# Moving every transfer of a log-softmax backward kernel from the sync engine's queue to GpSimd's software queue

## The chip, the cores and the metric

The kernel runs on one core of one Trainium2 chip. The metric is device time in microseconds (us), lower is better. Most executions of one kernel agree within 0.3%. All runs quoted here were at full granted clock. A transfer (DMA) is spread over 16 transfer engines of the core; the trace does not name them, so "the first" and "the last" engine below are meant in order of arrival. "SP" is the sync engine (SyncE), "DVE" VectorE, "ACT" ScalarE, "POOL" GpSimd.

## The reference

```python
batch, seq_len, vocab = 8, 1024, 8192            # float32
softmax_x = np.exp(y)
sum_dy = np.sum(dy, axis=-1, keepdims=True)
return (dy - softmax_x * sum_dy).astype(np.float32)
```

It reads two tensors of 268 MB and writes one of the same size.

## The kernel before

The 8192 rows are handled in 32 groups of 256: each of the 128 partitions holds two neighbouring rows (R = 2) of D = 8192 columns. `dy` of a group is one 8 MB transfer, `y` is two of 4 MB, and the result is written over `dy` in SBUF and stored as one 8 MB transfer. There are two `dy` buffers and two `y` buffers, together 192 KB of each partition. So a `dy` load must wait until the store from the same buffer, two groups back, has landed.

```python
    dyp = ctx.enter_context(tc.tile_pool(name="dyp", bufs=2))
    yp = ctx.enter_context(tc.tile_pool(name="yp", bufs=R))

    def load_dy(g):
        dy_t = dyp.tile([P, R * D], fp32, name="dy_t")
        nc.sync.dma_start(out=dy_t[:], in_=dy_v[g])
        s_t = stats.tile([P, R], fp32, name="s_t")
        nc.vector.tensor_reduce(...)              # s_t = -sum of each row of dy, L47

    def load_y(g):
        for r in range(R):
            y_t = yp.tile([P, D], fp32, name="y_t")
            nc.sync.dma_start(out=y_t[:], in_=y_v[g][:, r * D : (r + 1) * D])

    def compute(dy_t, s_t, y_ts):                 # per row: two halves of 4096 columns
        ...
                nc.scalar.activation(e, e, EXP)   # L69
                nc.vector.scalar_tensor_tensor(   # dy += exp(y) * s_t, L70, "the product"
                    out=d, in0=e, scalar=s_t[:, r : r + 1], in1=d, op0=ALU.mult, op1=ALU.add
                )

    # ... loop: load_y(g); compute(g); load_dy(g + 1); store(g).
    # The last groups are handled a little differently.
```

All transfers go through one queue, in the order y, y, dy of the next group, store, and every engine works through its share of each transfer in that order (the packets of the trace come in it).

## Time and profile before

| | before |
|---|---|
| time, median of the first 4 runs | 1867.24 us |
| moved, rate over the span | 805.36 MB, 432 GB/s |
| one group's packets on one engine | 16 of 64 KB at 2.418 us and 16 of 32 KB at 1.213 us: 58.1 us |
| loop period | 58.08 us |

The page of the kernel before. The second line is the busy time of each compute engine, with its share of the span; the row of digits is the busy share of the transfer engines in 40 slices, in tenths (9 is 90% or more); the line that begins with q1 is the hardware queue, with its share of the 16 engines' time; the last three lines are groups of instructions, with busy time and mean ns of one, then idle time before them and what ended it.

```profile
span 1865.4 us, 712 instructions
DVE 1119.2 (60%) x160; ACT 457.1 (25%) x129; POOL 0.2 (0%) x4
...
DMA  9999999999999999999999999999999999999999
...
q1 hardware_dynamic: 18576, 805.31, 99.9%
...
L70 DVE SCALAR_TENSOR_TENSOR dy_t<-y_t,s_t,dy_t 128x4096 f32<-128x4096 f32 x128 | 568.1, 4481 | 490.3 <-ACT y_t L69 490.1
L69 ACT ACTIVATE y_t<-y_t 128x4096 f32<-128x4096 f32 x128 | 455.9, 3608 | 1375.6 <-DMA y_t<-in_y_dram 1375.6
L47 DVE TENSOR_REDUCE s_t<-dy_t 128x2 f32<-128x16384 f32 x32 | 551.0, 17220 | 232.1 <-DMA dy_t<-in_dy_dram 232.1
```

The transfer engines are busy from beginning to end and the compute engines are not. The idle times of the last three lines are waits for loads, directly or through ACT. The kernel is bound by the transfers.

The timeline of the kernel before in the middle of the run (start, length, engine, line, operation; in brackets how long the engine stood idle and for what):

```profile
977.93 8.88 DVE L70 SCALAR_TENSOR_TENSOR dy_t<-y_t,s_t,dy_t 128x4096 f32<-128x4096 f32 x2 [0.83 <-ACT y_t L69]
986.84 0.34 SPq L77 DMA_DIRECT2D out_dram<-dy_t  x1
987.28 0.86 SPq L60 DMA_DIRECT2D y_t<-in_y_dram  x2
993.56 17.22 DVE L47 TENSOR_REDUCE s_t<-dy_t 128x2 f32<-128x16384 f32 x1 [6.75 <-DMA dy_t<-in_dy_dram]
1012.91 0.33 SPq L45 DMA_DIRECT2D dy_t<-in_dy_dram  x1
...
1044.92 0.34 SPq L77 DMA_DIRECT2D out_dram<-dy_t  x1
```

The last products end at 986.81, the store is issued at once, the y loads of the next group behind it. The `dy` load ahead of them in the queue has landed in full only at 993.56, 6.75 us later, when the reduction starts. So the queue still holds work when the store joins it. The chain of waits of the same stretch repeats every 58.08 us; its largest pieces are these (start, length, what):

```profile
929.66 44.53 DMA y_t<-in_y_dram
...
987.75 44.52 DMA y_t<-in_y_dram
...
1045.83 44.52 DMA y_t<-in_y_dram
```

They are waits for y, but of a y load that stands in the queue behind the store: a wait for bandwidth and not for latency.

### The profile page before, as it was taken

The numbers are of one execution on the slowest core, as the hardware profiler recorded it, in microseconds if no ns is written. First come the engines' busy times: TensorE is split into PE (matmuls) and PEld (weight loads), VectorE is DVE, ScalarE is ACT, GpSimd is POOL, SyncE is SP. The second block draws the span as 40 slices with busy tenths as digits, with TensorE's granted clock in tenths as the row PEclk, the third lists the DMA queues.
The fourth block names the chain that finished last, engine by engine and source line by source line (L and its number), as shares of the span: only waits on it lengthen the run. The fifth ranks groups of instructions, "written<-read, shape, count | busy, mean of one in ns | idle before, by whom it ended". The sixth has DMA issues, their size and how long they took to land.

```text
span 1865.4 us, 712 instructions
## 1 busy us (share of the span) xinstructions
DVE 1119.2 (60%) x160; ACT 457.1 (25%) x129; POOL 0.2 (0%) x4
## 2 busy tenths in 40 slices
DVE  5675555755557555575555755657656576565664
ACT  2123321233212332123321233212332113331132
POOL 0000000000000000000000000000000000000000
DMA  9999999999999999999999999999999999999999
GB/s 427 416 434 431 443 433 422 435 437 436 427 433 431 440 430 434 431 429 441 433 437 425 433 442 431 434 425 436 438 434 433 428 434 437 437 431 430 429 435 396
DMA packets 18582, 805.36 MB, mean 432 GB/s; under 512 B 2064, under 2 KB 2064, under 8 KB 2064
## 3 DMA queue, kind: packets, MB, share of 16 engines
q1 hardware_dynamic: 18576, 805.31, 99.9%
q14 instruction: 6, 0.05, 0.0%
HBM read 536.87 MB, written 268.44 MB: 432 GB/s over the span
## 4 chain that ended last, share of the span: by engine, by line
DMA 74%; DVE 17%; ACT 6%; SPq 1%; issue 1%; DVEq 0%; ACTq 0%
DMA y_t<-in_y_dram 69%; DVE dy_t L70 15%; ACT y_t L69 6%; DMA dy_t<-in_dy_dram 3%; DVE s_t L47 2%; DMA out_dram<-dy_t 1%; SPq L60 1%; SPq L77 1%; DVEq L122 0%; ACTq L69 0%; DVEq L70 0%
## 5 line engine op out<-in xcount | busy, mean ns | idle before, releaser
L70 DVE SCALAR_TENSOR_TENSOR dy_t<-y_t,s_t,dy_t 128x4096 f32<-128x4096 f32 x128 | 568.1, 4481 | 490.3 <-ACT y_t L69 490.1
L69 ACT ACTIVATE y_t<-y_t 128x4096 f32<-128x4096 f32 x128 | 455.9, 3608 | 1375.6 <-DMA y_t<-in_y_dram 1375.6
L47 DVE TENSOR_REDUCE s_t<-dy_t 128x2 f32<-128x16384 f32 x32 | 551.0, 17220 | 232.1 <-DMA dy_t<-in_dy_dram 232.1
L69 ACT ACT_TABLE_LOAD x1 | 1.3, 1283 | 0.7 <-PEq L111 0.7
L111 POOL MEMSET const-bfloat16-1.0<- 128x1 bf16 x1 | 0.1, 102 | 0.0
L111 POOL MEMSET const-uint8-127<- 128x1 uint8 x1 | 0.1, 102 | 0.0
L111 POOL MEMSET const-float32-1.0<- 128x1 f32 x1 | 0.1, 99 | 0.0
L111 POOL MEMSET const-float32-0.0<- 128x1 f32 x1 | 0.1, 98 | 0.2 <-issue 0.2
## 6 DMA issues: line engine op xcount, KB each, us to landing
y_t<-in_y_dram SPq DMA_DIRECT2D x64, 4096.0 KB, 35.9
out_dram<-dy_t SPq DMA_DIRECT2D x2, 4096.0 KB, 22.6
dy_t<-in_dy_dram SPq DMA_DIRECT2D x32, 38.7
out_dram<-dy_t SPq DMA_DIRECT2D x31, 26.1
```

The lines of the kernel that those rows point to most:

```text
L47: nc.vector.tensor_reduce(out=s_t[:], in_=dy_t[:].rearrange("p (r d) -> p r d", r=R), axis=mybir.AxisListType.X, op=ALU.add, negate=True,)
L60: nc.sync.dma_start(out=y_t[:], in_=y_v[g][:, r * D : (r + 1) * D])
L69: nc.scalar.activation(e, e, EXP)
L70: nc.vector.scalar_tensor_tensor(out=d, in0=e, scalar=s_t[:, r : r + 1], in1=d, op0=ALU.mult, op1=ALU.add)
L77: nc.sync.dma_start(out=out_v[g][:, k * w : (k + 1) * w], in_=dy_t[:, k * w : (k + 1) * w])
L111: nc = _bacc.Bacc("TRN2", target_bir_lowering=False, num_devices=1)
```

## The change

All three kinds of transfer are issued from GpSimd. Their descriptors (what tells an engine what to copy) are then written by software on GpSimd and not by hardware. Bytes, order, sizes and buffers stay.

```diff
-        nc.sync.dma_start(out=dy_t[:], in_=dy_v[g])
+        nc.gpsimd.dma_start(out=dy_t[:], in_=dy_v[g])
...
-            nc.sync.dma_start(out=y_t[:], in_=y_v[g][:, r * D : (r + 1) * D])
+            nc.gpsimd.dma_start(out=y_t[:], in_=y_v[g][:, r * D : (r + 1) * D])
...
-            nc.sync.dma_start(
+            nc.gpsimd.dma_start(
                 out=out_v[g][:, k * w : (k + 1) * w], in_=dy_t[:, k * w : (k + 1) * w]
             )
```

## The prediction

> **What bounds the kernel now.** The transfers. The page of the kernel before shows 805.36 MB in a span of 1865.4 us (432 GB/s), the hardware queue at 99.9% of the 16 engines' span, and a 9 in every slice of the DMA row, against 60% for VectorE and 25% for ScalarE. The trace's packets: 8064 of 65,536 bytes at a median of 2.418 us and 8448 of 32,768 bytes at 1.213 us. One group of 256 rows costs each engine 16 of the former and 16 of the latter, 58.1 us; the chain of waits repeats every 58.08 us. The engines have almost no gap.
>
> **How the loop keeps the queue full (timeline, 930 to 1050 us).** A group's store is issued at 986.84, after VectorE's last product; the dy load ahead of it in the queue lands only at 993.56. So the store has 6.7 us of backlog in front of it. The y loads follow within 1.2 us and have the store's 19.4 us in front. The next dy load waits for that store to land (1012.91) and has two y loads, 19.4 us, in front. The chain of waits names y loads for 69% of the span, but this is queueing, not latency.
>
> **What the change does.** It removes 129 issues from SyncE, 0.33 to 0.4 us each in the timeline, and adds 129 on GpSimd, which otherwise does 0.2 us of work. Bytes, row lengths, order and buffers stay. I expect the same packets at the same 2.42 and 1.21 us, under a software queue. The Trainium skill, "DMA: Bandwidth & Descriptors", section "Latency and other measured facts", gives about 1 us to the first byte on the software path and 0.6 us on the hardware path; this trace has no software transfer to check it. Estimated from this page, the extra 0.4 us per issue, and even 2 us, is under the 6.7 us of the tightest place, so the steady loop hides it. It shows only at the first load (0.5 to 3 us, with any first-use cost on GpSimd) and at the end.
>
> "SBUF — State Buffer" in the skill describes descriptor writing locked out while VectorE runs a two-port fast mode. I take no instruction here to be in one (the product takes 4.44 us for 4096 columns, the reduction 1.05 ns per column). And the issues fall where VectorE is idle: the store and y loads in the 6.75 us between last product and reduction, the dy load after the reduction ended (1010.8).
>
> **Sum.** 1866.9 + about 2 at start and end + 0 to 0.1 us per group for fetching descriptors from memory (0 to 3) = about 1870 us; 8 times in 10 within 1863 to 1892. Faster by over 2%: 0.01; within 2%: 0.85; slower by over 2%: 0.14.
>
> **What would show it right.** A software queue with near 18,576 packets of the same sizes, 9 in all DMA slices, about 431 GB/s; a loop period of 58.1 to 58.3 us; the reduction's wait for dy still near 6.75 us; store issue to landing still near 26 us.
>
> **What would make it wrong.** Packets cut smaller, so that a fixed cost per packet appears; some of the 16 engines slower than others, because they also serve the descriptor rings; a stall at each transfer's end before the next begins (four transfers per group: 0.3 us each would be 2%); descriptor writing over 6 us per transfer, so that the store reaches a dry queue; or a long first use of GpSimd's software. Each would show as gaps or longer packets in the DMA row, and each makes it slower, not faster.

## The result, and the profile after

The kernel after takes 1878.38 us in the median (1877.34 to 1879.35, 4 runs) against 1867.24 us (1866.81 to 1868.3, 4 runs): 11.1 us more. The ratio is 1.0059 with a 95% interval of 1.0041 to 1.0076, so it is the same within 2%, but the small loss is real. Ratios here are the mean time of one kernel's fast runs over that of the other's of the same rounds, so not quite the ratio of the medians.

The page of the kernel after, the same lines and the one of the store's issue:

```profile
span 1877.6 us, 712 instructions
DVE 1119.2 (60%) x160; ACT 457.1 (24%) x129; POOL 68.4 (4%) x133
...
DMA  9999999999999999999999999999999999999998
...
q0 software_dynamic: 18576, 805.31, 99.7%
...
L70 DVE SCALAR_TENSOR_TENSOR dy_t<-y_t,s_t,dy_t 128x4096 f32<-128x4096 f32 x128 | 568.2, 4481 | 491.2 <-ACT y_t L69 491.0
L69 ACT ACTIVATE y_t<-y_t 128x4096 f32<-128x4096 f32 x128 | 455.9, 3608 | 1386.8 <-DMA y_t<-in_y_dram 1386.8
L47 DVE TENSOR_REDUCE s_t<-dy_t 128x2 f32<-128x16384 f32 x32 | 551.0, 17220 | 242.0 <-DMA dy_t<-in_dy_dram 242.0
L77 POOL DMA_DIRECT2D out_dram<-dy_t x33 | 17.7, 538 | 1009.3 <-DVE dy_t L70 1009.3
```

The queue is now the software queue q0. It holds the same bytes in the same 18,576 packets, at 99.7%. Compute is unchanged. The digits of the transfer row still read 9: the loss is too small for this view. The waits moved a little: ACT's for y by 11.2 us (1375.6 to 1386.8), the reduction's for dy by 9.9 us (232.1 to 242.0).

The chain of waits is of little use here. Its summary by engine in the kernel after begins:

```profile
issue 85%; DMA 9%; POOL 3%; DVE 2%; ACT 0%; POOLq 0%; DVEq 0%; PEldq 0%; ACTq 0%
```

"Issue" means time for which the view found nothing to wait for. GpSimd's issues now stand in the chain as instructions, and the view does not follow the waits of GpSimd's own queue further. It is not a new cost.

The timeline after, at about the same place:

```profile
932.33 0.54 POOL L77 DMA_DIRECT2D out_dram<-dy_t  x1 [31.49 <-DVE dy_t L70]
...
939.88 17.22 DVE L47 TENSOR_REDUCE s_t<-dy_t 128x2 f32<-128x16384 f32 x1 [7.85 <-DMA dy_t<-in_dy_dram]
...
982.32 8.88 DVE L70 SCALAR_TENSOR_TENSOR dy_t<-y_t,s_t,dy_t 128x4096 f32<-128x4096 f32 x2 [0.84 <-ACT y_t L69]
991.50 0.54 POOL L77 DMA_DIRECT2D out_dram<-dy_t  x1 [31.50 <-DVE dy_t L70]
992.02 1.05 POOL L60 DMA_DIRECT2D y_t<-in_y_dram  x2
998.13 17.22 DVE L47 TENSOR_REDUCE s_t<-dy_t 128x2 f32<-128x16384 f32 x1 [6.92 <-DMA dy_t<-in_dy_dram]
1017.68 0.53 POOL L45 DMA_DIRECT2D dy_t<-in_dy_dram  x1 [24.61 <-DMA out_dram<-dy_t]
...
1049.72 0.54 POOL L77 DMA_DIRECT2D out_dram<-dy_t  x1 [31.51 <-DVE dy_t L70]
...
1056.86 17.22 DVE L47 TENSOR_REDUCE s_t<-dy_t 128x2 f32<-128x16384 f32 x1 [7.44 <-DMA dy_t<-in_dy_dram]
```

Two things are to be seen. The last products end at 991.20 (982.32 + 8.88); the store's record begins 0.30 us later (0.03 before) and lasts 0.54 us (0.34 before). And the stores no longer come every 58.08 us: 932.33, 991.50, 1049.72 are 59.2 and 58.2 us apart.

For the rest, the trace's packets and semaphore updates were read directly (differences are taken before rounding). Split at the first load's landing and at the last store's landing, the span of the two profiled runs falls into three parts:

| us | before | after | difference |
|---|---|---|---|
| start, to the first dy load's landing | 22.7 | 23.7 | +0.9 |
| from there to the last landing ("the loop") | 1841.9 | 1852.2 | +10.3 |
| from the last landing to the end | 0.8 | 1.7 | +0.9 |

The start, from the timelines of before and then after:

```profile
0.73 0.38 SPq L45 DMA_DIRECT2D dy_t<-in_dy_dram  x1
...
22.74 17.22 DVE L47 TENSOR_REDUCE s_t<-dy_t 128x2 f32<-128x16384 f32 x1 [22.74 <-DMA dy_t<-in_dy_dram]
...
61.83 17.22 DVE L47 TENSOR_REDUCE s_t<-dy_t 128x2 f32<-128x16384 f32 x1 [4.09 <-DMA dy_t<-in_dy_dram]
```

```profile
1.27 0.67 POOL L45 DMA_DIRECT2D dy_t<-in_dy_dram  x1 [0.83 <-PEq L122]
...
23.69 17.22 DVE L47 TENSOR_REDUCE s_t<-dy_t 128x2 f32<-128x16384 f32 x1 [23.69 <-DMA dy_t<-in_dy_dram]
...
62.44 17.22 DVE L47 TENSOR_REDUCE s_t<-dy_t 128x2 f32<-128x16384 f32 x1 [3.76 <-DMA dy_t<-in_dy_dram]
```

GpSimd issues its first transfer 0.54 us later than SP did, and from issue to landing it takes 22.42 us and not 22.01, 0.41 us more. The Trainium skill, "DMA: Bandwidth & Descriptors", section "Latency and other measured facts", gives about 1 us to the first byte on the software path and 0.6 us on the hardware path; the difference of 0.4 us agrees. From the start of the issue's record to the first packet the traces have 1.38 us and 1.01 us: the same difference, at levels 0.4 us above the page's.

The loop is where the time went. The 16 semaphore updates of a transfer show when each engine has finished its share. Here are the 16 landings of some dy loads and of the store between them (us, in order of arrival, the first three, the ninth and the last four):

```
before, dy    990.3  990.3  990.4 ...  991.4 ...  992.0  992.0  993.5  993.5
after,  dy    934.7  934.7  934.8 ...  935.2 ...  936.7  938.8  938.9  939.9
after,  out   954.4  954.5  954.6 ...  954.8 ...  956.0  958.1  958.2  959.2
after,  dy    992.9  993.1  993.2 ...  993.3 ...  994.9  996.9  997.0  998.1
```

The engines are not in step. In both kernels a few lag: by 3.2 us before and by 5.2 us after, in these groups. The "6.75 us of work ahead of the store" was read from the last engine. The first engine has finished its dy share at 990.3 before, 3.5 us after the store was issued (986.84), and after the change at 934.7 and 992.9, only 2.4 and 1.4 us after the issue (932.33 and 991.50).

Which packets got longer? Each engine's packets follow each other without a gap, so they can be strung together (97% or more of them fall into place), and the time over the usual length (2.418, 1.213 or 0.612 us by size) can be summed by place. Means over the 16 engines, us in the whole run; "loop" is the time from the first to the last landing of the same profiled run:

```
run             loop    dy: last packet  dy: others   store: last packet  store: others   y
before          1841.9       1.62           1.38             0.08              0.18        0.70
after           1852.2       3.54           1.07             5.28              0.55        1.34
```

Almost all of the growth is in the last packet of a dy load, where the engine's next packet is of a store, and in the last packet of a store, where the next is of a load: the places where an engine turns from reading device memory to writing it, or back. In the kernel before such packets were long too, but mostly early: of its 103 packets of 64 KB that took over 0.1 us more than usual, 74 lie in the first 420 us. Then the engines had drifted apart into a pattern that stayed: from 877 us on, the step from the last y landing to the last dy landing is 19.34 to 19.36 us in every group. After the change there are 308 such packets, to the end of the run, and in the second half that step alternates from group to group between 19.34 to 19.52 us and 19.65 to 20.79 us.

The packets were strung a second time, so that every one found its place. This gave 3.86 and 5.46 us for the two large numbers of the kernel after, and two things more. First, in the kernel before no store's first packet follows a gap of over 0.005 us, and the earliest starts 2.7 us after the store's issue. In the kernel after the earliest starts 1.1 us after it, and 15 of the 496 first packets follow a gap of over 0.1 us, the longest of 1.0 us: a leading engine did run dry now and then. These gaps sum to 0.4 us per engine only, and hw_later (below) has none of them, so the time did not go there. Second, in the second half of the kernel after (from 930 us) the long last packets of dy loads belong to the four engines that finish last (45 of their 64 are over 0.1 us too long, against 3 of 192 of the other twelve), and the long last packets of stores to the other twelve (127 of 192, against none of 64). So what is lost at the end of a load is lost on the laggards, and not on the leaders, for which the store came late.

### The profile page after: what moved, and what is told of

Same layout as the page of the kernel before. It is cut to its first block, busy times and chain, and to the rows that moved or that the text cites. A ratio compares the mean times of both kernels' runs of the same rounds, so it can differ in the third digit from the quotient of the medians.

```text
span 1877.6 us, 712 instructions
## 1 busy us (share of the span) xinstructions
DVE 1119.2 (60%) x160; ACT 457.1 (24%) x129; POOL 68.4 (4%) x133
## 3 DMA queue, kind: packets, MB, share of 16 engines
q0 software_dynamic: 18576, 805.31, 99.7%
## 4 chain that ended last, share of the span: by engine, by line
issue 85%; DMA 9%; POOL 3%; DVE 2%; ACT 0%; POOLq 0%; DVEq 0%; PEldq 0%; ACTq 0%
DMA dy_t<-in_dy_dram 3%; DMA out_dram<-dy_t 3%; DMA y_t<-in_y_dram 2%; POOL y_t L60 2%; DVE s_t L47 1%; DVE dy_t L70 1%; POOL out_dram L77 1%; POOL dy_t L45 1%; ACT y_t L69 0%; POOLq L122 0%; POOLq L60 0%; POOLq L77 0%; DVEq L70 0%; PEldq L122 0%; ACTq L69 0%
## 5 line engine op out<-in xcount | busy, mean ns | idle before, releaser
L69 ACT ACTIVATE y_t<-y_t 128x4096 f32<-128x4096 f32 x128 | 455.9, 3608 | 1386.8 <-DMA y_t<-in_y_dram 1386.8
L47 DVE TENSOR_REDUCE s_t<-dy_t 128x2 f32<-128x16384 f32 x32 | 551.0, 17220 | 242.0 <-DMA dy_t<-in_dy_dram 242.0
L77 POOL DMA_DIRECT2D out_dram<-dy_t x33 | 17.7, 538 | 1009.3 <-DVE dy_t L70 1009.3
L45 POOL DMA_DIRECT2D dy_t<-in_dy_dram x32 | 17.1, 534 | 741.4 <-DMA out_dram<-dy_t 740.6
L60 POOL DMA_DIRECT2D y_t<-in_y_dram x64 | 33.6, 530 | 33.8 <-DVE dy_t L70 31.0
## 6 DMA issues: line engine op xcount, KB each, us to landing
out_dram<-dy_t POOLq DMA_DIRECT2D x31, 26.1
```

Source lines behind the costliest of these rows:

```text
L45: nc.gpsimd.dma_start(out=dy_t[:], in_=dy_v[g])
L47: nc.vector.tensor_reduce(out=s_t[:], in_=dy_t[:].rearrange("p (r d) -> p r d", r=R), axis=mybir.AxisListType.X, op=ALU.add, negate=True,)
L60: nc.gpsimd.dma_start(out=y_t[:], in_=y_v[g][:, r * D : (r + 1) * D])
L77: nc.gpsimd.dma_start(out=out_v[g][:, k * w : (k + 1) * w], in_=dy_t[:, k * w : (k + 1) * w])
```

## Experiments

Two theories. **LATE**: the software's issue comes later, too late for the engines that lead, and this upsets the pace of the 16 engines. **SOFTWARE**: descriptors written by software slow the transfers whenever they are issued. The edits below are shortened, and `nc.X` in them is the issuing engine of the kernel that is edited. Twelve kernels ran, on three chips; ratios are to the kernel before, on the same chip and in the same rounds. Each profile shows one execution; those of hw_late and sw_split fell on the slowest of their five.

### Stores earlier, in halves: sw_split (from after) and hw_split (from before)

```diff
 def compute(...):
     for r in range(R):
         ...products of row r...
+        store row r of the group from here         # nc.X.dma_start of 128 x 8192
 # loop: the dy load of the next group is issued before compute, which keeps the queue's order
-    store(g)                                       # both rows in one transfer
```

> Software queue, but each half of a store (one of the two rows) is issued as soon as that row's products are done, so the store reaches the queue about 9.7 us earlier; the order of the bytes in the queue is unchanged. In the kernel after, the leading transfer engine finishes the dy load 5 us before the last one, so only about 2.3 us of work are left in front of it when the store is issued. Theory LATE (the software issue comes too late for the leading engines, which upsets the pace): the loss goes, 1867 to 1871 us, step between groups 58.1 us, and few 64 or 32 KB packets over 100 ns above their usual time. Theory SOFTWARE (fetching software-written descriptors slows the transfers whenever they are issued): it stays 8 to 12 us above the split hardware kernel of the same call, 1874 to 1880 us.

> Control: the same early half stores on the hardware queue. Both theories: 1862 to 1868 us; 31 more transfers cost nothing that shows.

Measured: sw_split 1874.45 us (1873.91 to 1876.8, 5 runs), ratio 1.0035 (1.0023 to 1.0048). hw_split 1868.82 us (1868.66 to 1870.13), ratio 1.0004 (0.9991 to 1.0016). Both correct. The early software store gives back some of the loss and not all. Neither theory foresaw this: the time lies within what SOFTWARE expected (1874 to 1880 us) and above LATE's 1867 to 1871, but the distance to hw_split is 5.6 us and not 8 to 12. The stores' last packets are back to normal (table below, 0.01 us), the dy loads' last packets are not (3.30 us), and the last engine falls 7.7 us behind the first by the end, against 3.5 us in hw_split.

### Stores later on the hardware queue: hw_late, hw_later, hw_late_small (all from before)

```diff
 def store(g, dy_t, parts=1):
+    if g < G - 2:
+        tail = dy_t[:, R * D - 1024 :]             # 3072 in hw_later, 256 in hw_late_small
+        nc.vector.tensor_copy(out=tail, in_=tail)
```

The copy writes what was there. The store must wait for it, and so must the y loads behind the store; it runs while VectorE would be idle.

> Kernel before (hardware queue), with the store held back by a copy of the last 1024 columns of its tile onto themselves on VectorE, an estimated 0.6 to 1.2 us, about as late as GpSimd issues it. LATE: 1872 to 1880 us, with the same alternating loss of about 1 us in every other group as in the kernel after. SOFTWARE: 1866 to 1868 us, as before.

> As the previous run with 3072 columns, an estimated 1.8 to 3.5 us late; the y loads behind the store come late by as much. LATE: more than the previous run, 1876 to 1900 us. SOFTWARE: still within 3 us of before as long as the last engine never runs dry (6.7 us of slack).

> Kernel before with a copy of only 256 columns ahead of the store, about 0.28 us, the delay that the trace of the kernel after shows between the last product and GpSimd's issue. LATE with a graded loss: 1869 to 1874 us. LATE with a threshold between 0.3 and 0.7 us: 1867 to 1869 us. SOFTWARE: 1867 to 1869 us.

Timeline of hw_late:

```profile
981.52 8.88 DVE L70 SCALAR_TENSOR_TENSOR dy_t<-y_t,s_t,dy_t 128x4096 f32<-128x4096 f32 x2 [0.84 <-ACT y_t L69]
990.44 0.69 DVE L78 COPY dy_t<-dy_t 128x1024 f32<-128x1024 f32 x1
991.16 0.34 SPq L81 DMA_DIRECT2D out_dram<-dy_t  x1
991.60 1.32 SPq L60 DMA_DIRECT2D y_t<-in_y_dram  x2
997.16 17.22 DVE L47 TENSOR_REDUCE s_t<-dy_t 128x2 f32<-128x16384 f32 x1 [6.03 <-DMA dy_t<-in_dy_dram]
```

The copy takes 0.69 us, the store is issued 0.76 us after the last product, and the reduction still waits 6.0 us or more for the dy load (from the second group on): the queue as a whole is never dry. The copy took 1.76 us in hw_later and 0.29 us in hw_late_small.

Measured: hw_late 1875.88 us (1872.38 to 1878.11, 5 runs), ratio 1.0036 (1.0022 to 1.0049). hw_later 1878.07 us (1876.72 to 1881.0, 5 runs), ratio 1.0054 (1.0042 to 1.0067). hw_late_small 1870.39 us with a wide scatter: 1868.73, 1867.01, 1877.06, 1872.78, 1872.06, 1868.14. All correct. On the hardware queue, with no software descriptor anywhere, a store that is 0.7 us late costs 8 us in the median, and the trace shows the same pattern as the kernel after: the dy step alternates, in the second half, between 19.35 and 19.9 to 20.6 us, and the long packets stand in the same two places. Later than that costs little more. With 0.3 us some executions are disturbed and some are not.

### Loads alone: loads_hw (from before) and loads_sw (from after)

```diff
             if g < G - 2:
-                store(g, cur[0])
                 cur = nxt
```

> The kernel before without the stores of the first 30 groups (wrong result on purpose), so the queue holds loads alone and no engine changes from reading to writing device memory in the loop. Both theories: the packet sum, 2 x 19.36 us per group for 31 groups plus start and end, about 1300 us, with almost no packet above its usual time.

> The same on the software queue; the y loads are still issued only some 6 us before the last dy load lands. Theory SWITCH (what is lost is lost where an engine's last packet of one direction meets other engines already on the other direction; a late issue and the software queue only change how often): within 2 us of loads_hw, all of it at the start and end, packets as in loads_hw. Theory FETCH (reading software-written descriptors slows packets or leaves gaps at any transfer's end): 0.1 us or more per group, 1303 to 1310 us.

Measured: loads_hw 1287.35 us (1287.13 to 1287.68, 4 runs), loads_sw 1292.16 us (1291.8 to 1292.51). Their outputs are wrong, which doesn't matter for the times. Both lie below the level expected (about 1300), which was an estimate. They are 4.8 us apart, and by the total alone that would have fitted FETCH. But it does not lie in the stream of transfers: from the first to the last landing they take 1261.8 and 1262.3 us. The start differs by 0.9 us, and the end by 3.9: from the last landing to the end of the span it is 0.9 and 4.8 us, because GpSimd is the last to reach the final barrier (in loads_sw its DRAIN ends 4.1 us after the last landing, and every other engine waits for it). From the two pages, hardware then software queue:

```profile
span 1285.4 us, 622 instructions
...
q1 hardware_dynamic: 14256, 553.65, 99.8%
```

```profile
span 1290.6 us, 622 instructions
...
q0 software_dynamic: 14256, 553.65, 99.5%
```

The software queue moves loads at the same rate, packet for packet: a dy load takes 19.4 us in both but for two groups, which are 0.5 to 1 us slower in both, and the lag of the last engine is 2.2 us in both. Theory FETCH is refuted for loads alone. The timeline of loads_sw shows one thing more:

```profile
507.24 17.67 DVE L70 SCALAR_TENSOR_TENSOR dy_t<-y_t,s_t,dy_t 128x4096 f32<-128x4096 f32 x4
...
516.41 0.53 POOL L60 DMA_DIRECT2D y_t<-in_y_dram  x1 [28.94 <-DVE dy_t L70]
...
525.73 0.53 POOL L45 DMA_DIRECT2D dy_t<-in_dy_dram  x1
```

GpSimd's record at 516.41 lies within VectorE's four products (507.24 to 524.91) and takes 0.53 us, as long as the one at 525.73, when VectorE was idle. The Trainium skill, "SBUF — State Buffer", section "SBUF: two separate sides", describes descriptor writing that is locked out while VectorE runs a two-port fast mode; no such lock-out shows in this record.

### The store earlier by another way: sw_yhalf (from after) and hw_yhalf (from before)

```diff
-        nc.X.dma_start(out=y_t[:], in_=y_v[g][:, r * D : (r + 1) * D])
+        # row 1 as two loads of 4096 columns, row 0 as before
+        for c in range(0, D, CD if r == R - 1 else D):
+            w = CD if r == R - 1 else D
+            nc.X.dma_start(out=y_t[:, c : c + w], in_=y_v[g][:, r * D + c : r * D + c + w])
```

> Kernel after with whole stores, but the second y row of a group is loaded as two halves, so its products end, and the store is issued, an estimated 4 us earlier. LATE: as the split stores on the software queue, 1873 to 1876 us, and the last packet of a store no longer runs over its usual time (0 to 0.5 us per engine in all, 5.3 in the kernel after). If instead the size of the store transfers was what helped in the split: no gain, 1877 to 1880 us, and the stores' last packets stay long.

> Control on the hardware queue: 1866 to 1869 us, both theories.

Timeline of sw_yhalf:

```profile
970.24 17.67 DVE L74 SCALAR_TENSOR_TENSOR dy_t<-y_t,s_t,dy_t 128x4096 f32<-128x4096 f32 x4 [15.50 <-ACT y_t L73]
988.21 0.54 POOL L81 DMA_DIRECT2D out_dram<-dy_t  x1 [30.55 <-DVE dy_t L74]
988.74 1.56 POOL L62 DMA_DIRECT2D y_t<-in_y_dram  x3
995.68 17.22 DVE L47 TENSOR_REDUCE s_t<-dy_t 128x2 f32<-128x16384 f32 x1 [7.76 <-DMA dy_t<-in_dy_dram]
```

The four products now run back to back, and the last one ends 7.76 us ahead of the reduction and not 6.75: the store is 1.0 us earlier against the dy load. The estimate of 4 us in the expectation was wrong, because VectorE becomes the limit of that stretch. One microsecond was enough.

Measured: sw_yhalf 1872.94 us (1872.57 to 1874.37, 5 runs), ratio 1.0026 (1.0013 to 1.0039). hw_yhalf 1870.39 us (1869.6 to 1871.43, 5 runs), ratio 1.0011 (0.9997 to 1.0024). The control hw_yhalf missed its expected 1866 to 1869 us by 1.4 us. The loops of the two profiled runs take 1844.4 us on the software queue and 1844.9 us on the hardware queue. What is left between them, 2.6 us in the medians, is the start (0.9) and the end (3.0 and 0.8 us after the last landing).

### Late again: sw_yhalf_late (from sw_yhalf, copy of 1536 columns) and hw_yhalf_late (from hw_yhalf, copy of 1024)

The edits are those of hw_late, on top of the half load.

> The kernel with the half y load (software queue, 1872.9 us), its store now held back again by a copy of 1536 columns, about 0.95 us by the two copies measured, so about as late as in the kernel after. LATE: the loss comes back, 1877 to 1882 us, with long last packets of stores (3 to 7 us per engine). If the half load helped for another reason: 1872 to 1875 us.

> The same half load on the hardware queue with the 0.69 us copy that cost 8 us by itself: the net issue is then about 0.3 us earlier than in the kernel before. LATE: no loss, 1868 to 1872 us. If the copy cost by itself and not through lateness: 1876 to 1880 us.

Measured: sw_yhalf_late fell into two kinds of execution: 1872.87, 1873.34, 1872.98 (as without the copy) and 1879.19, 1878.32, 1880.12 (as LATE expected); the profile was of an undisturbed one, so the long store packets that LATE expected were not seen. hw_yhalf_late 1869.96 us (1869.67 to 1870.83, 5 runs), ratio 1.0008 (0.9996 to 1.002), all undisturbed. So the same 0.69 us copy that cost 8 us costs nothing where the store has 1 us in hand, and taking that microsecond back from the software kernel brings the loss back, in half of the executions.

### Another order of groups: sw_evens (from after)

```diff
+    at = [*range(0, G, 2), *range(1, G, 2)]
 ...                                                # dy_v[g], y_v[g], out_v[g] become
+    dy_v[at[g]], y_v[at[g]], out_v[at[g]]
```

> Kernel after with the groups in the order 0, 2, 4 ... 30, 1, 3 ... 31, so that neighbouring transfers are 16 MB apart in device memory and not 8. In the kernel after, the long last dy packets come in every other group. If they follow the parity of the address: in all groups of one half and none of the other, or gone (1868 to 1874 us). If they follow the SBUF buffer or are a swing that feeds itself: every other group still, 1876 to 1881 us.

Measured: 1869.66, 1882.85, 1878.49, 1875.16 us; ratio 1.0042 (1.002 to 1.0064). The profile fell on the first, which is undisturbed, so it does not tell what the alternation follows: inconclusive for its question. It tells something else: the software kernel, with whole stores issued 0.3 us after the products, can run its loop in 1842.9 us (kernel before: 1841.9) and come out at 1869.66 us, some 2 us above the kernel before.

### All runs in one table

Read from the profiled runs as above (long packets: us over the usual length, mean of the 16 engines; the loop ends with the slowest engine, so the two need not move alike). "Store at" is the start of the store's issue after the last product's end.

```
run             store at   loop    dy: last  store: last  end after last landing
before            0.03    1841.9     1.62       0.08        0.8
hw_late_small     0.35    1843.7     2.10       0.29        0.8
hw_late           0.76    1852.9     4.21       5.53        0.8
hw_later          1.82    1852.1     2.74       6.93        0.8
hw_split           -      1843.6     2.36       0.00        0.9
hw_yhalf          -1.0    1844.9     1.83       0.05        0.8
hw_yhalf_late     -0.3    1844.5     1.45       0.31        0.8
after             0.30    1852.2     3.54       5.28        1.7
sw_split           -      1848.6     3.30       0.01        2.9
sw_yhalf          -0.7    1844.4     1.77       0.21        3.0
sw_yhalf_late      0.3    1844.5     1.39       0.56        3.0
sw_evens           0.30   1842.9     2.18       0.10        1.7
loads_hw           -      1261.8     0.13        -          0.9
loads_sw           -      1262.3     0.30        -          4.8
```

(For the half-load kernels "store at" is given relative to where the products end in the kernels without the half load, that is less the 1.0 us gained.)

And the executions, counted as disturbed by limits that were set after the results were seen: where they lie over 1870 us on the hardware queue, over 1872 us on the software queue (for the longer start and end), and over 1872 and 1875 us in the half-load kernels on the two queues (the undisturbed ones lie at 1869.6 to 1871.4 and 1872.6 to 1874.4):

```
kernel before, all rounds of the three calls     5 of 29
hardware queue, store 0.3 us late                3 of 6
hardware queue, store 0.7 us late                5 of 5
hardware queue, store 1.8 us late                5 of 5
hardware queue, half load, with and without copy 0 of 10
software queue (after)                           4 of 4
software queue, other order of groups            3 of 4
software queue, half load, store 1 us earlier    0 of 5
the same, late again                             3 of 6
hardware queue, stores in halves (hw_split)      1 of 5
software queue, stores in halves (sw_split)      5 of 5
```

Even the kernel before has such executions (1870.58 to 1873.43 us), and the one of hw_split is at its limit (1870.13 us). On the hardware queue a later store makes them more frequent and stronger. It is not the only thing that does: the stores of sw_split are early, and all five of its executions count.

No run beat the kernel before: hw_split, the nearest, is the same within its interval.

## Why the prediction was right or wrong

- **"Bytes, row lengths, order stay; the same packets at the same 2.42 and 1.21 us."** Right: 18,576 packets, the same medians. Loads alone run as fast on either queue (1262.3 and 1261.8 us), so the 0 to 0.1 us per group allowed for fetching descriptors were 0.02 there.
- **"At the start and end about 2 us."** Right: 0.9 + 0.9 us in the kernel after. The end was not understood, though: it is GpSimd's own arrival at the last barrier, and in other kernels it came up to 3.9 us later than with the hardware queue.
- **"The tightest place is 6.7 us, so the steady loop hides it", 0 to 3 us.** This is the mis-sized term: the loop lost 10.3 us. Two errors went into it. The 6.7 us were read in the middle of the run and at the last of the 16 engines; the first engine had 3.5 us there, and the first group's store has 4.1 us even at the last engine (the wait of 4.09 us at 61.83). And it took for granted that lateness costs nothing as long as no engine runs dry. The queue as a whole did not run dry in hw_late either (99.9% of the engines' span, and the reduction waited 6.0 us or more for its load), and it still lost 8 us: packets get longer where the engines turn from reading to writing and back, and with a later store this goes on to the end of the run. From the end of the products to the flow of data, the software issue is by estimate about 0.7 us later: 0.27 us in the start of the record (0.30 against 0.03) and the 0.41 us more from issue to landing of the first load. That is the lateness of hw_late, which cost about the same.
- **"Each would show as gaps or longer packets in the DMA row."** Half right: they are longer packets, but only the packet records show them. The row of digits reads 9 throughout.
- **"Loop period 58.1 to 58.3 us"**: wrong, 58.5 us in the mean ((1817.4 - 62.4) / 30, from the dy landings), alternating. **"The reduction's wait near 6.75"**: 6.75 to 8.2 from the third group on. **"Store issue to landing near 26 us"**: right, 26.1.
- The total, 1878.38 us, lies inside 1863 to 1892 and within 2%, but 8 us above the sum of about 1870: it is inside because the range had room for a cause that the text did not foresee, and that is luck.

What is shown: the loss in the loop is not a cost that software descriptors always bring (loads_sw; sw_yhalf against hw_yhalf; the undisturbed execution of sw_evens), and a late store, with the y loads behind it, is enough to bring a loss of this size on (hw_late, hw_later; sw_yhalf against sw_yhalf_late). What is only argued: that the leading engines, with 3.5 us and less, are the ones that decide; they are where the store arrives late, but the long dy packets are on the laggards. What stays open: by what mechanism a packet lengthens where the directions change, why the same kernel settles in one execution and not in the next, why every other group is hit, and why sw_split, whose stores are early, still has long dy packets (2.7 us more than hw_split beyond its longer start and end, by the medians: 5.63 - 0.85 - 2.05). So a part of the loss that the software queue brings without a late store is not ruled out.

## What to carry to other kernels

Read the slack in a full queue at the first transfer engine to finish too, and not at the last alone: the landings of the 16 engines can be several microseconds apart (3.2 and 5.2 us here). In a transfer-bound loop that alternates loads and stores, a store that comes 0.7 us later can cost ten times as much over the run although the queue as a whole never runs dry, so test a suspected lateness by delaying the good kernel as well as by hurrying the bad one. Look at several executions, since such a loop may settle in some and not in others; and if transfers must be issued from GpSimd, try to give the store a microsecond in hand, which took most of the loss out of the loop in sw_yhalf (1844.4 us against 1852.2, and 1841.9 before; stores in halves, sw_split, took out less).

## What the Trainium skill lacked or had wrong

- "DMA: Bandwidth & Descriptors", "SWDGE vs HWDGE vs iDMA", calls the hardware path faster in setup and does not say how the two compare in a long stream of large transfers. Here they are within 0.5 us: 1261.8 and 1262.3 us for the same loads.
- "DMA: Bandwidth & Descriptors", "Measured (HBM→SBUF, 128 partitions, SWDGE, issued from GpSimd)": the table's rates do not follow from its sizes and times (16 MB in 79.0 us is 212 GB/s, the table says 425). On this software queue an 8.39 MB load took 19.35 us, 433 GB/s.
- The same page, "Latency and other measured facts", guesses that two engines, 7 and 15, are usually slower because of the software descriptor rings, and not on the hardware path. The hardware queue has laggards too: 3.5 us at the end of the kernel before, and 2.2 us in both loads-only kernels. Which engines they are, this trace does not name.
- No page says that packets lengthen where the engines turn from loads to stores and back: up to 1.3 us over 2.418 us for one packet of the kernel after, and 8.8 us per engine over its run (3.54 + 5.28).
- No page gives the end of a kernel that issues from GpSimd: 1.7 to 4.8 us from the last landing to the end of the span, against 0.8 to 0.9 us with the hardware queue.
